# Norm products spread over five steps, and the weight sums of four blocks moved from GpSimd to VectorE

## The chip, the cores and the metric

The kernel runs on one core of a Trainium2 chip. The metric is device time in microseconds (us): 1652.0 us is the median of three runs of the kernel before (1651.32 to 1652.88). Less is better. Five engines execute side by side, each its own list of instructions in order: TensorE (PE, matmuls), VectorE (DVE), ScalarE (ACT), GpSimd (POOL) and SyncE (SP), which here only issues transfers.

## The reference, cut to what matters

One layer of a decoder trunk on a sequence of 1024 tokens with 1024 features, all in float32:

```
mod = silu(c) @ w_ada + b_ada            # six vectors of 1024: shifts, scales, gates
h = rmsnorm(x) * g_mix * (1 + sc1) + sh1
proj = h @ w_in                          # 1024 -> 4640 columns: q, k, v of a dilated attention,
                                         # latents of a second attention, and two gates
x = x + gt1 * (sig(gate_a)*U_a(A) + sig(gate_b)*U_b(B)) @ w_o
h = rmsnorm(x) * g_ffn * (1 + sc2) + sh2
x = x + gt2 * (silu(h @ w_gate) * (h @ w_up)) @ w_down
out = rmsnorm(x) * g_final
```

The change lies in the making of `h` and in the first part of `h @ w_in`.

## The kernel before, in words

**Precision.** A float32 operand is held as two parts, a rounded high part (`hi`, made by ScalarE, L83) and the rest (`lo`, made by VectorE, L84); a product is three matmuls (hi x hi, hi x lo, lo x hi). Each weight tile and each activation tile thus costs one ScalarE cast and one VectorE subtraction before TensorE may use it. The tiles of the split weights are called `Wop`.

**Fast products.** The big matrix products use Strassen's scheme: weight and activation are cut into 2 x 2 quarters, and 7 products replace 8. Each of the 7 needs a sum of weight quarters and a sum of activation quarters. Activation sums are made once (class `Rights`, subtractions at L280, splits into the tiles `cell`). Weight sums are made for every block of weights in `Strassen.left`, by `Strassen.sum` (L192), on the engine named by the class attribute `summer`, which is GpSimd (`POOL`): four sums of 128 x 512 for a block, from `Wraw` (the loaded weights) into `Wsum`. Two of them (S1 and S2) feed products 4 and 5, one feeds 6, one feeds 2; products 0, 1 and 3 use a quarter as it is. The 7 products go in the order 0, 1, 5, 4, 6, 3, 2, each 12 matmuls (L222) into a PSUM bank `bk`. A bank is read by VectorE (L235 adds a base into `x`, L388 makes a finished quarter of the output) before the next product may overwrite it.

**The opening loop** (k from 0 to 7, from L488). For every eighth of the features it loads the modulation weights, makes the norm of the first 512 tokens, multiplies `x` by it (`unit`, L447, "norm products"), applies scale and shift (`affine`, L450), and runs plain products of the first half of 768 columns of `w_in` (six groups of 128, L520). These cover products 0 and 1 of the first six blocks and one output quarter.

**The pair loop** (`for g in range(9)`, L704). The 18 blocks of `w_in` are taken two at a time: pair 0 is blocks 0 and 1, pair 1 blocks 2 and 3, and so on. Blocks 0 to 3 give k and q of the dilated attention. A pair loads its two `Wraw` (1 MB each, L184; there are two buffers, so a load waits until the block before has used its buffer up), and runs products 5, 4, 6, 3, 2 for both. Blocks 0 to 5 come from the opening loop with a base and skip 0 and 1; so do blocks 6 and 7. Between products, chores are put in: the bias table of the attention (one-hot loads L598, matmuls L604, VectorE L605, store L606 into `rxd`, and then eight DRAM-to-DRAM copies of 128 x 1152, L609, into `rxx`), the rotary angles (positions loaded by L613, cast by L618 and on), and the modulation sums (loads L159 from `wada`, VectorE L677, with the condition row `sg` loaded by L666).

**What sets the order.** The program is written in the order above, but a planner places the instructions: it plays the program through with its own clock and gives each engine a list, with hints such as `tc.high_priority` and `tc.issue_after`. After that each engine executes its list strictly in order; an instruction that waits holds everything behind it on its engine.

Of the kernel before, what the change touches and what calls it, by code (L numbers as in the profile page):

```python
# [44 lines left out]
def layer_kernel(ctx: ExitStack, tc: tile.TileContext, xT, c, pos, relT, wada, bada, gains, gq, gkv,  # L45
# [3 lines left out]
    ACT, DVE, PE, POOL, SP = nc.scalar, nc.vector, nc.tensor, nc.gpsimd, nc.sync  # L49
# [5 lines left out]
    def pool(stack, name, bufs=1, **kw):  # L55
        if kw.get("space") is not DRAM:
            kw["reuse_waits"] = "tile"
        return stack.enter_context(tc.tile_pool(name=name, bufs=bufs, **kw))
# [61 lines left out]
    def rms_rows(y, rb, nb=4):  # L120
        for j in range(nb):
            rows_ins[0] = PE.transpose(rb[:, j * P:(j + 1) * P], y[:, j:j + 1].to_broadcast([P, P]), ident)
        return rb
# [279 lines left out]
    with ExitStack() as s0:  # L403
        gwr = pool(s0, "gwr", 3, side="right")
        adap = pool(s0, "adap", 6, side="right")
        early = pool(s0, "early", 1, side="right")
        sqp = pool(s0, "sqp", 3, side="right")
        SQ = lambda: sqp.tile([P, H], F32, name="sq")
        condb = early.tile([P, D], F32, name="condb")
        ssq = [early.tile([P, H], F32, name=f"ssq{i}") for i in range(2)]  # L410
        cr = early.tile([1, D], F32, name="crow")
        badc1 = early.tile([P, 8], F32, name="badc1")
        onesr = early.tile([1, P], F32, name="onesr")
        crow = [cr[:, hsl[hf]] for hf in range(2)]
        for hf in range(2):
            ld(crow[hf], c[:, hsl[hf]])
        for k in range(8):
            ld(x[k][0], xT[k][:, hsl[0]])
        ld(badc, bada)
        ld(gn, gains)  # L420
        DVE.memset(ones1, 1.0)
        DVE.memset(epsc, EPS)
        ACT.activation(warm, ones1, AF.Silu)
        DVE.memset(onesr, 1.0)
        POOL.memset(ident, 0.0)
        POOL.affine_select(ident, ident, pattern=[[-1, P]], compare_op=OP.not_equal, fill=1.0,
                           base=0, channel_multiplier=1)
        sq_ins = [None]

        def square(hf, k):  # L430
            if k == 0:
                ACT.activation(ssq[hf], x[k][hf], AF.Square)
            else:
                q = SQ()
                sq_ins[0] = ACT.activation(q, x[k][hf], AF.Square)
                DVE.tensor_add(ssq[hf], ssq[hf], q)

        def rms(hf):
            ps = trb()
            y = rms_cols([ssq[hf]], D, ps, root=True)  # L440
            rows = rms_rows(y, ps)
            if hf == 1:
                ACT.activation(warm, epsc, AF.Sigmoid)
            return rows

        def unit(k, hf, rb):
            DVE.tensor_mul(x[k][hf], x[k][hf], rb)  # L447

        def affine(out, k, hf):
            return ACT.activation(out, x[k][hf], AF.Identity, bias=modc[:, k:k + 1], scale=Acol[:, k:k + 1])  # L450

        def mod_in(m, k):
            j = m * 8 + k
            t = adap.tile([P, D], F32, name="ada")
            ld(t, wada[j])
            DVE.tensor_tensor_reduce(t, t, condb, 1.0, 0.0, OP.mult, OP.add, modc[:, j:j + 1])
            if m == 1:
                DVE.scalar_tensor_tensor(Acol[:, k:k + 1], modc[:, j:j + 1], badc1[:, k:k + 1], gn[:, k:k + 1],
                                         op0=OP.add, op1=OP.mult)
            else:  # L460
                DVE.tensor_add(modc[:, j:j + 1], modc[:, j:j + 1], badc[:, j:j + 1])

        for k in range(8):
            square(0, k)
            if k == 0:
                for hf in range(2):
                    ACT.activation(crow[hf], crow[hf], AF.Silu)
                    st(cnd[:, hsl[hf]], crow[hf])
                    ps = bank()
                    PE.matmul(ps, onesr, crow[hf], start=True, stop=True)  # L470
                    ins = ACT.copy(condb[:, hsl[hf]], ps)
        with tc.issue_after(sq_ins[0].ins):
            ACT.activation(warm, epsc, AF.Sqrt)
        DVE.tensor_scalar(badc1, badc[:, 8:16], 1.0, None, op0=OP.add)

        def kr_mm(w, t, first, last):
            PE.matmul(pkr[:64], w, t[:, 0], start=first, stop=False, skip_group_check=True)
            PE.matmul(pkr[:32], w[:, :32], t[:, 1], start=False, stop=last, skip_group_check=True)

        def kr_out(t, tmp, hf):  # L480
            ACT.copy(tmp, pkr[32:64])
            DVE.tensor_add(t, pkr[:32], tmp)
            st(krr[:, hsl[hf]], t)

        pss = [bank() for _ in range(NGP)]
        sg = []
        gates = ExitStack()
        for k in range(8):  # L488
            mod_in(1, k)
            mod_in(0, k)  # L490
            if k == 0:
                rb0 = rms(0)
                pkr = trb()
            raw = gwr.tile([P, GW], F32, name="gwraw")
            last = ld(raw, wg0[k])
            if 2 <= k <= 5:
                for kk in (2 * (k - 2), 2 * (k - 2) + 1):
                    with tc.issue_after(last.ins):
                        last = ld(x[kk][1], xT[kk][:, hsl[1]])
            hi = gwr.tile([P, GW + 32], F32R, name="gwh")  # L500
            lo = gwr.tile([P, NGP * P], F32R, name="gwl")
            ACT.copy(hi[:, :GW], raw)
            DVE.tensor_sub(lo, raw[:, :NGP * P], f32(hi[:, :NGP * P]))
            DVE.tensor_sub(hi[:, GW:], raw[:, NGP * P:], f32(hi[:, NGP * P:GW]))
            if k < 4:
                unit(2 * k, 0, rb0)
                unit(2 * k + 1, 0, rb0)
            t = R1.ops[k // 4][k % 4]
            hi_ins = affine(t[:, 0], k, 0)
            affine(x[k][0], k, 0)  # L510
            lo_ins = DVE.tensor_sub(t[:, 1], x[k][0], f32(t[:, 0]))
            if k == 0:
                gates.enter_context(tc.issue_after(hi_ins.ins))
                gates.enter_context(tc.issue_after(lo_ins.ins))
            for j in range(NGP):
                s = slice(j * P, j * P + P)
                if k == 6 and j == 2:
                    gates.enter_context(tc.issue_after(rows_ins[0].ins))
                for n, (wi, ti) in enumerate(((hi, 0), (hi, 1), (lo, 0))):
                    PE.matmul(pss[j], wi[:, s], t[:, ti], start=k == 0 and n == 0, stop=k % 4 == 3 and n == 2,  # L520
                              skip_group_check=True)
            kr_mm(hi[:, NGP * P:], t, k == 0, k == 7)
            if k == 3:
                for j in range(NGP):
                    t = SG()
                    ACT.copy(t, pss[j])
                    sg.append(t)
            if 2 <= k <= 5:
                for kk in (2 * (k - 2), 2 * (k - 2) + 1):
                    square(1, kk)  # L530
            if k == 5:
                with tc.high_priority(offset=400):
                    rb1 = rms(1)
            if k >= 6:
                for kk in range(4 * (k - 6), 4 * (k - 6) + 4):
                    unit(kk, 1, rb1)
        for k in range(8):
            affine(x[k][1], k, 1)
    gates.close()
    gates.enter_context(tc.issue_after(last.ins))  # L540
    prs = [In(j, load=False, base=sg[j]) for j in range(NGP)]
    q6 = In(6, load=False)
    q6.load01()
    tq = pool(ctx, "tq", side="right")
# [177 lines left out]
    with ExitStack() as s2:  # L722
# [293 lines left out]
        for u in range(64 + DEPTH):  # L1016
# [14 lines left out]
            for kp in range(w % 4 + 1) if w >= 0 else ():  # L1031
# [4 lines left out]
                if len(queue) > 2:  # L1036
                    q, k = queue.pop(0)
# [221 lines left out]
    for ci in range(NC):  # L1259
        for dd in range(2):  # L1260
            prs = [Down(2 * dd + e, ops, wnext[:, e]) for e in range(2)]
# [184 lines left out]
```

## Time and profile before

| | before |
|---|---|
| median of 3 runs | 1652.0 us |
| profiled execution, in all | 1657.39 us |
| its span | 1655.5 us |
| mean granted TensorE clock | 0.964 |
| TensorE matmul busy | 1533.7 us (93%) |
| VectorE busy | 1230.6 us (74%) |
| ScalarE busy | 829.9 us (50%) |
| GpSimd busy | 492.1 us (30%) |

Times in the profile are us from the start of its span. In a timeline a row has start, length, engine, line, operation, what is written and read, how many instructions are merged, and in brackets how long the engine was idle just before and what ended the wait. A table of waits has, for each pair of waiter and releaser, the total, the number of times, and the longest. A row of a stretch has its bounds and length, busy time (and count) of TensorE, its weight loads, VectorE, ScalarE and GpSimd, then the granted clock, the transfers' share of their 16 engines, and GB/s.

### The profile page before, as it was taken

How to read it: one execution, taken by the hardware profiler on the slowest of the kernel's cores; microseconds unless marked ns; L12 is line 12 of the kernel's file. 1: busy time of each engine (PE TensorE's matmuls, PEld its weight loads, DVE VectorE, ACT ScalarE, POOL GpSimd, SP SyncE). 2: the span in 40 equal slices, each digit the busy share in tenths (PEclk: the TensorE clock that was granted, in tenths of full speed). 3: DMA queues.
4: the chain of work that ended last, by engine and by line, in shares of the span. 5: the costliest groups of instructions: out<-in, count | busy, mean ns of one | idle time of the engine just before them, and what ended most of it. 6: DMA issues, size and time to landing. Idle time of an engine off the chain costs nothing.

```text
span 1655.5 us, 22260 instructions
## 1 busy us (share of the span) xinstructions
PE 1533.7 (93%) x7306; PEld 1278.2 (77%) x7306; DVE 1230.6 (74%) x2478; ACT 829.9 (50%) x1631; POOL 492.1 (30%) x470
## 2 busy tenths in 40 slices
PE   4988899999778998999999999999999999899996
PEld 2757678877567887899978887778888888788885
DVE  7887898576276766888876569677777677688887
ACT  5742425444366876878744446434444444222325
POOL 0142333223343545433200000423332332233323
PEclk8889999999888999999999999999999999999998
DMA  9439775467996987776376441554444447967512
GB/s 324 185 119 334 239 257 186 142 200 209 281 240 167 225 194 197 175 184 153 90 254 236 126 160 68 180 185 166 165 150 152 166 156 275 396 251 254 187 36 102
DMA packets 175364, 321.40 MB, mean 194 GB/s; under 512 B 36988, under 2 KB 72492, under 8 KB 170000
## 3 DMA queue, kind: packets, MB, share of 16 engines
q1 hardware_dynamic: 107088, 241.22, 42.9%
q0 software_dynamic: 48000, 42.04, 12.0%
q10 hardware_dynamic: 20160, 36.71, 5.9%
q8 instruction: 58, 0.95, 0.2%
q14 instruction: 58, 0.48, 0.1%
HBM read 222.20 MB, written 102.34 MB: 196 GB/s over the span
## 4 chain that ended last, share of the span: by engine, by line
PE 63%; DMA 14%; DVE 12%; ACT 4%; issue 4%; POOL 1%; SPq 0%; ACTq 0%; DVEq 0%; POOLq 0%
PE bk L222 40%; PE acc L894 4%; DMA cell<-ksd 4%; PE S L785 3%; PE bk L87 3%; PE pv L826 3%; PE bk L88 3%; PE bk L89 3%; DMA cell<-nqd 2%; PE tr L807 2%; DVE Wop L84 2%; DMA cell<-tod 1%; PE bk L520 1%; DMA cl<-wada 1%; DVE cell L84 1%
## 5 line engine op out<-in xcount | busy, mean ns | idle before, releaser
L222 PE MATMUL bk<-cell,Wop 128*128 128x512 f32 x4056 | 949.1, 396 | 40.1 <-DVE x L235 14.4
L222 PEld LDWEIGHTS bk<-cell,Wop 128*128 128x128 f32 x4056 | 772.3, 191 | 210.8 <-DVE Wop L84 9.8
L192 POOL TENSOR_TENSOR Wsum<-Wraw 128x512 f32<-128x512 f32 (+1 forms) x116 | 151.7, 1310 | 771.3 <-DVE Wop L84 369.6
L83 ACT CAST Wop<-Wsum 128x512 fp32r<-128x512 f32 (+1 forms) x241 | 129.9, 549 | 222.6 <-PE bk L222 168.7
L83 ACT CAST Wop<-Wraw 128x512 fp32r<-128x512 f32 (+2 forms) x182 | 107.5, 593 | 183.9 <-PE bk L222 101.2
L84 DVE TENSOR_TENSOR Wop<-Wsum,Wop 128x512 fp32r<-128x512 f32 (+1 forms) x241 | 156.4, 657 | 47.0 <-ACT Wop L83 46.2
L84 DVE TENSOR_TENSOR Wop<-Wraw,Wop 128x512 fp32r<-128x512 f32 (+2 forms) x182 | 130.6, 721 | 33.8 <-ACT Wop L83 31.4
L785 PE MATMUL S<-cell,cell 128*128 128x128 f32 (+8 forms) x480 | 120.1, 365 | 12.9 <-DMA cell<-ksd 8.3
L1248 DVE SCALAR_TENSOR_TENSOR x<-bk,modc,x 128x512 f32<-128x512 f32 x140 | 103.7, 748 | 35.9 <-PE bk L222 31.5
L792 ACT ACTIVATE P<-P,mx 128x512 f32<-128x512 f32 (+7 forms) x128 | 99.3, 778 | 35.8 <-DVE mx L787 22.5
L84 DVE TENSOR_TENSOR pl<-tr,ph 128x512 fp32r<-128x512 f32 (+1 forms) x160 | 98.4, 631 | 22.2 <-ACT ph L83 21.2
L894 PE MATMUL acc<-cell,w 128*128 128x512 f32 x408 | 112.2, 403 | 0.1
L807 PE MATMUL tr<-ident,P 128*128 128x128 f32 x576 | 94.5, 282 | 7.1 <-ACT P L795 6.4
L785 PEld LDWEIGHTS S<-cell,cell 96*128 96x128 f32 (+1 forms) x480 | 80.9, 197 | 21.9 <-DMA cell<-ksd 8.7
L192 POOL TENSOR_TENSOR Wsum<-Wraw,Wsum 128x512 f32<-128x512 f32 (+1 forms) x58 | 76.7, 1329 | 65.0 <-DVE Wop L84 62.8
L826 PE MATMUL pv<-ph,v 128*128 128x256 f32 (+1 forms) x320 | 88.2, 293 | 5.9 <-ACT ph L83 5.1
L87 PE MATMUL bk<-cell,Wop 128*128 128x512 f32 (+1 forms) x240 | 91.2, 380 | 1.9 <-ACT Wop L83 1.9
L83 ACT CAST ph<-tr 128x512 fp32r<-128x512 f32 (+1 forms) x160 | 83.3, 544 | 17.2 <-PE tr L807 14.4
L88 PE MATMUL bk<-cell,Wop 128*128 128x512 f32 (+1 forms) x240 | 90.8, 379 | 0.0
L89 PE MATMUL bk<-cell,Wop 128*128 128x512 f32 (+1 forms) x240 | 89.7, 378 | 0.0
L163 ACT COPY x<-bk 128x512 f32<-128x512 f32 x92 | 52.3, 584 | 68.7 <-PE bk L222 45.0
L894 PEld LDWEIGHTS acc<-cell,w 128*128 128x128 f32 x408 | 76.2, 193 | 13.0 <-DVE ev L925 0.3
(255 smaller groups left out, 2181.3 us busy)
## 6 DMA issues: line engine op xcount, KB each, us to landing
tod<-x ACTq DMA_DIRECT2D x140, 256.0 KB, 2.7
cell<-tod SPq DMA_DIRECT2D x70, 512.0 KB, 7.5
Wraw<-win SPq DMA_DIRECT2D x18, 1024.0 KB, 8.0
Wraw<-wgate SPq DMA_DIRECT2D x11, 1024.0 KB
Wraw<-wup SPq DMA_DIRECT2D x11, 1024.0 KB, 6.2
Wraw<-wdown SPq DMA_DIRECT2D x20, 512.0 KB, 4.1
ada<-wada SPq DMA_DIRECT2D x16, 512.0 KB, 6.8
cm<-wada SPq DMA_DIRECT2D x32, 256.0 KB, 3.3
```

Source lines behind the costliest of these rows:

```text
L83: ACT.copy(hi, src)
L84: eng.tensor_sub(lo, src, f32(hi))
L87: PE.matmul(ps, w[0], a[0], start=first, stop=False)
L88: PE.matmul(ps, w[0], a[1], start=False, stop=False)
L89: PE.matmul(ps, w[1], a[0], start=False, stop=last)
L192: self.summer.tensor_tensor(t, a, b, op=op)
L222: PE.matmul(ps, w[:, wi, k], t[k][:, ti], start=start and k == 0 and n == 0, stop=k == self.nk - 1 and n == 2, skip_group_check=True)
L785: anchor[0] = PE.matmul(s, q[:, i * P:i * P + P], k[:, c * wd:c * wd + wd], start=pi == 0, stop=pi == len(passes) - 1)
L807: anchor[0] = PE.transpose(tr[:, co:co + P], self.p[a][:, kb * P:kb * P + P], ident)
L826: anchor[0] = PE.matmul(pv[:, o if l else 0:], v[:, kk], p[:, l:r], start=kk == 0 and n == 0, stop=last and l > 0 and n == 1, skip_group_c ...
L894: PE.matmul(ps, w[wi][:, k0 + k], act(k, ai, hf), start=k == 0 and n == 0, stop=k == nk - 1 and n == 2)
L1248: DVE.scalar_tensor_tensor(xs, self.bk[name], modc[:, 40 + j:41 + j], xs, op0=OP.mult, op1=OP.add)
```

## The change

It has two parts. In the opening loop, `unit` for the first half of the tokens was called twice in each of the steps 0 to 3; now it is called for features (0, 1), (2), (3, 4), (5) and (6, 7) in the steps 0 to 4. And `summer` of blocks 0 to 3 is set to VectorE, so that their 16 sums at L192 are made by VectorE.

```diff
@@ -502,9 +502,8 @@
             ACT.copy(hi[:, :GW], raw)
             DVE.tensor_sub(lo, raw[:, :NGP * P], f32(hi[:, :NGP * P]))
             DVE.tensor_sub(hi[:, GW:], raw[:, NGP * P:], f32(hi[:, NGP * P:GW]))
-            if k < 4:
-                unit(2 * k, 0, rb0)
-                unit(2 * k + 1, 0, rb0)
+            for kk in ((0, 1), (2,), (3, 4), (5,), (6, 7), (), (), ())[k]:
+                unit(kk, 0, rb0)
             t = R1.ops[k // 4][k % 4]
             hi_ins = affine(t[:, 0], k, 0)
             affine(x[k][0], k, 0)
@@ -539,6 +538,8 @@
     gates.close()
     gates.enter_context(tc.issue_after(last.ins))
     prs = [In(j, load=False, base=sg[j]) for j in range(NGP)]
+    for q in prs[:4]:
+        q.summer = DVE
     q6 = In(6, load=False)
     q6.load01()
```

Because a planner places the instructions, more moves than the diff shows. Lines below 505 keep their numbers in the changed kernel, those from L508 to L541 are one lower, and those after it one higher (L618 becomes L619).

**VectorE's list in pair 0, at the first two L235.** `cell` tiles are activation splits, `Wop` weight splits, `x_1035` and `x_1057` the banks read for blocks 0 and 1. Before:

```order
L84 TENSOR_TENSOR Wop_1119<-Wsum_1117,Wop_1119 128x512
L84 TENSOR_TENSOR Wop_1143<-Wraw_1011,Wop_1143 128x512
L84 TENSOR_TENSOR cell9_986<-cl_279,cell9_986 128x512
L84 TENSOR_TENSOR Wop_1165<-Wraw_1013,Wop_1165 128x512
L84 TENSOR_TENSOR cell10_987<-cl_281,cell10_987 128x512
L605 SCALAR_TENSOR_TENSOR cl_1316<-tr_1319,cl_1316 8x512
L84 TENSOR_TENSOR cell11_988<-cm_283,cell11_988 128x512
L235 TENSOR_TENSOR x_1035<-bk_1022,sg_558 128x512
L235 TENSOR_TENSOR x_1057<-bk_1044,sg_560 128x512
```

And now:

```order
L84 TENSOR_TENSOR cell11_988<-cm_283,cell11_988 128x512
L606 SCALAR_TENSOR_TENSOR cl_1316<-tr_1319,cl_1316 8x512
L235 TENSOR_TENSOR x_1035<-bk_1022,sg_556 128x512
L235 TENSOR_TENSOR x_1057<-bk_1044,sg_558 128x512
L84 TENSOR_TENSOR Wop_1119<-Wsum_1117,Wop_1119 128x512
L84 TENSOR_TENSOR Wop_1143<-Wraw_1011,Wop_1143 128x512
L84 TENSOR_TENSOR Wop_1165<-Wraw_1013,Wop_1165 128x512
L192 TENSOR_TENSOR Wsum_1187<-Wraw_1011,Wsum_1017 128x512
L606 SCALAR_TENSOR_TENSOR cl_1468<-tr_1471,cl_1468 8x512
L192 TENSOR_TENSOR Wsum_1211<-Wraw_1013,Wsum_1039 128x512
```

Three weight splits that stood ahead of L235 stand behind it, two sums (L192) are behind it as well, and two others (not in these rows) ahead.

**TensorE's list at the same place**, product 6 of block 0 and the bias matmuls L604. Before:

```order
L222 MATMUL bk<-cell_948,Wop 128x512 x5
L222 MATMUL bk<-cell_969,Wop 128x512 x3
L222 MATMUL bk<-cell_970,Wop 128x512 x3
L222 MATMUL bk<-cell_971,Wop 128x512 x3
L222 MATMUL bk<-cell_972,Wop 128x512 x3
L222 MATMUL bk<-cell_969,Wop 128x512 x3
L222 MATMUL bk<-cell_970,Wop 128x512 x3
L222 MATMUL bk<-cell_971,Wop 128x512 x3
L222 MATMUL bk<-cell_972,Wop 128x512 x3
L604 MATMUL tr<-cl,rt 8x512
L604 MATMUL tr<-cl,rt 8x128
```

And now:

```order
L222 MATMUL bk<-cell_948,Wop 128x512 x5
L605 MATMUL tr<-cl,rt 8x512
L222 MATMUL bk<-cell_969,Wop 128x512 x3
L222 MATMUL bk<-cell_970,Wop 128x512 x3
L222 MATMUL bk<-cell_971,Wop 128x512 x3
L222 MATMUL bk<-cell_972,Wop 128x512 x3
L222 MATMUL bk<-cell_969,Wop 128x512 x2
L605 MATMUL tr<-cl,rt 8x128
```

The two bias matmuls stood behind both blocks' product 6; now one stands ahead of them and one among them.

**VectorE's list in pair 1**, around the second bank read of block 2 (`x_1340`). Before:

```order
L84 TENSOR_TENSOR Wop_1421<-Wsum_1419,Wop_1421 128x512
L84 TENSOR_TENSOR Wop_1445<-Wsum_1443,Wop_1445 128x512
L235 TENSOR_TENSOR x_1340<-bk_1246,sg_562 128x512
L388 TENSOR_TENSOR x_1342<-bk_1286,x_1340 128x512
L84 TENSOR_TENSOR x_1342<-x_1342,x_1344 128x512
L235 TENSOR_TENSOR x_1366<-bk_1268,sg_564 128x512
L388 TENSOR_TENSOR x_1368<-bk_1302,x_1366 128x512
L84 TENSOR_TENSOR x_1368<-x_1368,x_1370 128x512
L388 TENSOR_TENSOR x_1390<-bk_1246,sg_562 128x512
L618 CAST cl_1717<-cl_1717 128x128
```

And now:

```order
L84 TENSOR_TENSOR Wop_1445<-Wsum_1443,Wop_1445 128x512
L619 CAST cl_1717<-cl_1717 128x128
L235 TENSOR_TENSOR x_1340<-bk_1246,sg_560 128x512
L620 TENSOR_SCALAR cl_1717<-cl_1717,fq_69 128x128
L388 TENSOR_TENSOR x_1342<-bk_1286,x_1340 128x512
L621 TENSOR_SCALAR cl_1717<-cl_1717 128x128
```

The cast of the positions, which waits for their load, stood behind the reads of three banks; now it stands ahead of all of them. `x_1340` must be read before TensorE's product 3 of block 2 may start.

## The prediction

> **What bounds the kernel now.** I read the engine shares first, then TensorE's waits in the opening third, then the timelines of TensorE, VectorE and GpSimd there.
>
> ```profile
> PE 1533.7 (93%) x7306; PEld 1278.2 (77%) x7306; DVE 1230.6 (74%) x2478; ACT 829.9 (50%) x1631; POOL 492.1 (30%) x470
> ```
>
> TensorE is the bound on average, so the change can only pay where TensorE stands still. Between 60 and 330 us its waits are:
>
> ```profile
> PE bk L222 <- DVE x L235: 11.7, 3, 5.3
> PE bk L222 <- DVE Wop L84: 4.9, 1, 4.9
> ```
>
> The changed sums themselves appear nowhere in this table; VectorE does. TensorE's timeline (start, length, then idle before) places the waits:
>
> ```profile
> 103.20 1.65 PE L222 MATMUL bk<-cell,Wop 128*128 128x512 f32 x6
> 106.40 1.20 PE L222 MATMUL bk<-cell,Wop 128*128 128x512 f32 x4 [1.55 <-DVE cell L84]
> 112.90 8.19 PE L222 MATMUL bk<-cell,Wop 128*128 128x512 f32 x24 [5.30 <-DVE x L235]
> 121.02 1.24 PE L604 MATMUL tr<-cl,rt 32*8 32x512 f32 x4
> 122.19 38.93 PE L222 MATMUL bk<-cell,Wop 128*128 128x512 f32 x170
> 166.06 4.10 PE L222 MATMUL bk<-cell,Wop 128*128 128x512 f32 x10 [4.94 <-DVE Wop L84]
> 171.75 14.02 PE L222 MATMUL bk<-cell,Wop 128*128 128x512 f32 x60 [1.60 <-ACT Wop L83]
> 188.78 29.52 PE L222 MATMUL bk<-cell,Wop 128*128 128x512 f32 x122 [3.01 <-DVE x L235]
> 221.71 3.78 PE L222 MATMUL bk<-cell,Wop 128*128 128x512 f32 x8 [3.41 <-DVE x L235]
> ```
>
> The six gaps make 19.8 us, all inside the first eight blocks. The long row gives the price of a matmul, 38.93 / 170 = 0.229 us. After a long gap matmuls are slower: 24 took 8.19 where 5.50 is due (2.7 lost), 10 took 4.10 where 2.29 is due (1.8 lost). So a gap costs itself and about 2 us more. Pair 0 (blocks 0 and 1) has 120 matmuls: 48 lie before the 5.30 gap, 24 directly behind it, 48 at the head of the 170. Pair 1 is the next 120 of the 170, pair 2 starts with the last two. Hence pair 0 ends at 122.19 + 48 x 0.229 = 133.2 and the first product (12 matmuls) of pair 2 is complete at 171.75. That is my milestone.
>
> Why is L235 late? VectorE before it:
>
> ```profile
> 88.33 0.67 DVE L84 TENSOR_TENSOR Wop<-Wsum,Wop 128x512 fp32r<-128x512 f32 x1
> 88.93 0.67 DVE L280 TENSOR_TENSOR x<-x 128x512 f32<-128x512 f32 x1
> ...
> 100.37 1.40 DVE L84 TENSOR_TENSOR cell<-cm,cell 128x512 fp32r<-128x512 f32 x1
> 101.69 1.76 DVE L84 TENSOR_TENSOR cell<-x,cell 128x512 fp32r<-128x512 f32 x1
> ...
> 104.59 1.75 DVE L84 TENSOR_TENSOR cell<-chi,cell 128x512 fp32r<-128x512 f32 x1
> 106.27 1.77 DVE L84 TENSOR_TENSOR cell<-x,cell 128x512 fp32r<-128x512 f32 x1
> ...
> 112.18 1.27 DVE L235 TENSOR_TENSOR x<-bk,sg 128x512 f32<-128x512 f32 x2
> ```
>
> VectorE has no gap here: its 33 instructions from 88.33 to 112.18 start 0.60 apart (33 x 0.60 = 19.8), except four that are stretched by 0.73 + 1.09 + 1.08 + 1.10 = 4.0. GpSimd over the same time:
>
> ```profile
> 92.10 10.81 POOL L192 TENSOR_TENSOR Wsum<-Wraw 128x512 f32<-128x512 f32 x2 [23.83 <-DVE Wop L84]
> 104.13 3.36 POOL L192 TENSOR_TENSOR Wsum<-Wraw,Wsum 128x512 f32<-128x512 f32 x2 [1.23 <-DVE Wop L84]
> 114.36 1.43 POOL L192 TENSOR_TENSOR Wsum<-Wraw 128x512 f32<-128x512 f32 x1 [6.86 <-DMA Wraw<-win]
> ...
> 157.03 1.29 POOL L192 TENSOR_TENSOR Wsum<-Wraw 128x512 f32<-128x512 f32 x1 [17.92 <-DMA Wraw<-win]
> ```
>
> The stretched instructions lie exactly where GpSimd's four sums finish and run. Two sums from 92.10 need 10.81 us instead of 2 x 1.43 while VectorE is dense: the two engines exclude each other, first GpSimd waits, then VectorE.
>
> **The change part by part.** *Norm products.* The instruction order of all five engines is the same with and without this part alone, because the planner had already put them two, then six, into VectorE's queue. It costs and brings 0.
>
> *First eight sums (pair 0).* Four move into VectorE's queue at 58 to 67 us, 4 x 0.60 = 2.4, in the places where that queue waits for ScalarE; the eight norm products that follow wait for the same row transposes, and I take 0 (bounds -1 and +1). Two more fall between 88.33 and L235, two behind it. Ahead of L235 the order now has 32 instructions, not 33, since three weight splits went behind it: 88.33 + 32 x 0.60 = 107.6, and GpSimd has nothing left to run. L235 is done at 108.3 instead of 112.85, and TensorE restarts there: **-4.5**. Bounds: -5.3 (the whole gap) and -0.6 (one instruction fewer, the stretches come from something else). The bias matmul L604 that now stands ahead of that restart waits for a one-hot load that is issued when the split of cell9_986 ends, near 105.3; I count it as in time.
>
> With 1.8 lost to the slower clock the 24 matmuls take 7.3, L604's remaining part 0.4, then 48 x 0.229 = 11.0: pair 0 ends at 127.0 instead of 133.2.
>
> *Next eight sums (pair 1).* Their 4.8 us fall where VectorE has had pauses, but each of the first two waits in VectorE's queue for its weight load. Queued behind the first is L235 of block 1, which TensorE needs for its product 3, near 121.9.
>
> ```profile
> 109.31 0.35 SPq L184 DMA_DIRECT2D Wraw<-win  x1
> ...
> 128.42 2.71 SPq L609 DMA_DIRECT2D rxx<-rxd  x4
> ...
> 145.21 0.33 SPq L184 DMA_DIRECT2D Wraw<-win  x1
> 146.00 0.63 SPq L613 DMA_DIRECT2D cl<-pos  x1
> ```
>
> That load took 109.31 to 114.36, 5.05 us. It can now be issued when the fourth sum of block 0 is made, 111.4, and lands near 116.5: 5 us in hand, cost 0 (bound +3).
>
> *What moves with it.* The bias matmuls no longer stand behind the 24, so the bias table's eight big copies (L609) start near 121, 7 us earlier. In the new order the cast L618 of the positions stands *ahead* of L235 of block 2 (x_1340); before, the cast stood seven places behind that L235.
>
> ```profile
> 147.00 0.69 DVE L235 TENSOR_TENSOR x<-bk,sg 128x512 f32<-128x512 f32 x1 [1.30 <-PE bk L222]
> ...
> 157.15 1.25 DVE L618 CAST cl<-cl 128x128 f32<-128x128 int32 x1 [4.00 <-DMA cl<-pos]
> 130.00:145.00 15.00, 15.00 (x68) 12.40 (x67) 13.69 (x24) 5.40 (x9) 4.59 (x3) 1.00 0.97 341
> ```
>
> So TensorE's product 3 of block 2 will wait for the positions. The transfers are saturated there (last row: stretch 130 to 145, share 0.97, 341 GB/s). Positions were issued 17.6 us after the first copy and landed 11.15 later, behind a 1 MB weight load that now stands after them (1.05 MB / 341 GB/s = 3.1). New landing: 121 + 17.6 + 11.15 - 3.1 = 146.7; x_1340 is done 1.25 + 0.69 later, at 148.6. TensorE wants it at 127.0 + 72 x 0.229 = 143.5. A **new gap of 5.1**, plus 1.8 of slow clock. Bounds: no gap (landing before 141.6), and 15.6 (landing at 157.15 as before).
>
> *Pair 2.* Pair 1 ends at 148.6 + 1.8 + 48 x 0.229 = 161.4. Pair 2's weight load (issued 145.21, landed 157.03 before) is issued when the last copy has landed, near 147, with less ahead of it; it takes between 5.05 and 11.8, then two sums of 1.3 and a split pair of 1.3 follow: ready between 156 and 162.7. The gaps of 4.94 and 1.60 thus mostly vanish, and the milestone comes at 161.4 + 2.75 = 164.2, or 165.5 at the late end, instead of 171.75: -7.6 to -6.2.
>
> *Behind it* VectorE is dense up to the L235 of 221.71 and GpSimd still makes the sums there. Same work, same interference: 0, bounds -3 and +3. From 221.71 on TensorE runs dense, so what is gained by then is kept.
>
> **Sum:** I take **-6.5**. The profiled execution (1655.5 span, 1657.4 in all) would become 1650.9; it lies 5.4 above the median of the runs, 1652.0, which becomes **1645.5**.
>
> **The rivals.**
>
> *Slower: the positions land too late.* From the landing T the milestone is T + 1.94 + 1.8 + 11.0 + 2.75 = T + 17.5, so the change loses from T = 154.3. For: the queue is full, and the two broadcast loads (L666) that VectorE also waits for now stand among the copies. Against: 7.6 us of margin. With T as before, 157.15, the milestone is 174.6, +2.9; with two broadcast waits at 2 us more, about +5: **1657**.
>
> *No change: VectorE pays what GpSimd saved.* 16 x 0.60 = 9.6 is added to a queue that is dense from 88 to 112 and from 160 to 222, against stretches of 4.0 that I can show for four sums, at most 16 x 1.1 = 17.6 in all; near 9 the two cancel, the dense stretch to 221.71 ends where it did, and the time is **1652**. For: the last two gaps there wait for VectorE, not for data. Against: none of the added sums lies behind 160. The Trainium skill says this outright: "Perfetto Trace Analysis", Optimizing Scalar/DVE Operations, holds that moving work between GpSimd and VectorE might not help, as they share an SBUF read port. By that rule the result is this rival's 1652; the rows agree on the sharing (92.10 for 10.81), but also show that the price falls on the engine that is late.
>
> *Larger gain: positions in time.* With T below 141.6 the new gap is gone, pair 1 ends at 154.5 and pair 2 waits only for its weights (156 or later): milestone near 159.5, -12: **1640**.
>
> **How the numbers follow.** Forecast (-3.3 to -10) 0.46, larger gain 0.12, no change 0.22, slower 0.20. A measurement of this kernel cannot tell less than 0.2% (3.3 us) from nothing. So faster 0.58, same 0.22, slower 0.20. The range takes in most of the larger gain and of the slow case, 1639 to 1656; the forecast's own is 1642 to 1649.
>
> **What would show it.** Right: no L192 on GpSimd before about 155; VectorE's splits near 100 to 107 all at 0.67; L235 near 108; the gap of 5.30 down to about 2.5; a new TensorE gap near 144 released by L235 with the L618 cast just before it; the gap at 161 gone. Wrong: stretched VectorE instructions without GpSimd beside them; VectorE waiting for `Wraw<-win` at 115 to 122 while TensorE stands; or the gaps before 189 and 222 growing by what was gained.

## The result, and the profile after

The changed kernel takes 1644.1 us (median of 6 runs, 1637.6 to 1647.3) where the kernel before takes 1652.4 on the same chip (6 runs, 1650.4 to 1654.1): ratio **0.9939**, 95% interval 0.9922 to 0.9956. It is faster by about 8 us; the forecast was 1645.5.

The two profiled executions must not simply be subtracted. That of the kernel before took 1657.4, 5.0 above its median; that of the changed kernel took 1637.6 (span 1635.4), 6.5 below its median. So 11.5 of the 19.8 us between them is the luck of two executions.

First the engine totals of the changed kernel (busy us, share of the span, instructions):

```profile
PE 1522.3 (93%) x7306; PEld 1266.9 (77%) x7306; DVE 1227.3 (75%) x2494; ACT 829.1 (51%) x1631; POOL 460.1 (28%) x454
```

Sixteen instructions went from GpSimd (470 to 454) to VectorE (2478 to 2494). GpSimd is busy 32 us less. VectorE is busy 3.3 us *less* with sixteen instructions more; two executions of one program differ by up to 6.7 there (1230.6 before, 1237.3 with the norm products alone), so the number says only that it is no busier. TensorE's timeline after (start, length, then idle before and what ended it; line numbers from L508 on differ by one from those before):

```profile
106.59 1.01 PE L605 MATMUL tr<-cl,rt 32*8 32x512 f32 x2 [1.89 <-DMA cl<-onehot]
107.71 5.03 PE L222 MATMUL bk<-cell,Wop 128*128 128x512 f32 x14
...
112.98 29.78 PE L222 MATMUL bk<-cell,Wop 128*128 128x512 f32 x130
148.53 17.05 PE L222 MATMUL bk<-cell,Wop 128*128 128x512 f32 x66 [5.77 <-DVE x L235]
165.84 12.53 PE L222 MATMUL bk<-cell,Wop 128*128 128x512 f32 x54 [0.27 <-DVE Wop L84]
180.88 28.02 PE L222 MATMUL bk<-cell,Wop 128*128 128x512 f32 x122 [2.50 <-DVE x L235]
212.34 64.90 PE L222 MATMUL bk<-cell,Wop 128*128 128x512 f32 x285 [3.45 <-DVE x L235]
```

The gap of 5.30 us at 112.9 is gone: TensorE goes on at 107.71. A new gap of 5.77 stands at 148.53. Those of 4.94 and 1.60 before pair 2 have shrunk to 0.27. VectorE's and GpSimd's timelines tell why:

```profile
106.89 1.27 DVE L235 TENSOR_TENSOR x<-bk,sg 128x512 f32<-128x512 f32 x2
...
142.26 0.69 DVE L678 CUSTOM_DVE_ANT_0 cm<-cm,sg 128x512 f32<-128x512 f32 x1 [4.02 <-DMA sg<-cnd]
...
147.55 0.23 DVE L619 CAST cl<-cl 128x128 f32<-128x128 int32 x1 [2.52 <-DMA cl<-pos]
147.70 0.68 DVE L235 TENSOR_TENSOR x<-bk,sg 128x512 f32<-128x512 f32 x1
```

```profile
153.17 1.29 POOL L192 TENSOR_TENSOR Wsum<-Wraw 128x512 f32<-128x512 f32 x1 [151.86 <-DVE cl L624]
```

VectorE's L235 pair comes at 106.89, not at 112.18, and GpSimd makes its first sum at 153.17. At 147.70 stands the L235 of block 2 (x_1340), right behind the cast of the positions that waited for its load, and, five microseconds earlier, a product for the modulation (L678) that waited 4.02 for a broadcast load.

### The profile page after: what moved, and what is told of

Same layout as the page of the kernel before. It is cut to its first block, busy times and chain, and to the rows that moved or that the text cites. A ratio compares the mean times of both kernels' runs of the same rounds, so it can differ in the third digit from the quotient of the medians.

```text
span 1635.4 us, 22253 instructions
## 1 busy us (share of the span) xinstructions
PE 1522.3 (93%) x7306; PEld 1266.9 (77%) x7306; DVE 1227.3 (75%) x2494; ACT 829.1 (51%) x1631; POOL 460.1 (28%) x454
## 4 chain that ended last, share of the span: by engine, by line
PE 49%; DMA 5%; DVE 5%; ACT 3%; issue 2%; POOL 1%; ACTq 0%; DVEq 0%; POOLq 0%; SPq 0%
PE bk L222 30%; PE acc L895 3%; PE S L786 3%; PE bk L87 3%; PE bk L89 3%; PE bk L88 3%; PE pv L827 2%; PE tr L808 2%; DMA vbd<-ev 2%; DMA tod<-x 1%; DMA cell<-tod 1%; DVE Wop L84 1%; DMA x<-x1d 1%; DVE cell L84 0%; DVE P L788 0%
## 5 line engine op out<-in xcount | busy, mean ns | idle before, releaser
L222 PE MATMUL bk<-cell,Wop 128*128 128x512 f32 x4056 | 938.0, 392 | 32.3 <-DVE x L235 14.4
L222 PEld LDWEIGHTS bk<-cell,Wop 128*128 128x128 f32 x4056 | 763.5, 189 | 201.4 <-issue 13.2
L192 POOL TENSOR_TENSOR Wsum<-Wraw 128x512 f32<-128x512 f32 (+1 forms) x108 | 131.5, 1220 | 800.0 <-DVE Wop L84 334.0
L786 PE MATMUL S<-cell,cell 128*128 128x128 f32 (+8 forms) x480 | 119.5, 364 | 11.2 <-DMA cell<-ksd 7.0
L192 POOL TENSOR_TENSOR Wsum<-Wraw,Wsum 128x512 f32<-128x512 f32 (+1 forms) x54 | 69.4, 1291 | 59.8 <-DVE Wop L84 57.7
L895 PEld LDWEIGHTS acc<-cell,w 128*128 128x128 f32 x408 | 75.0, 190 | 12.7 <-DVE ev L926 0.3
```

The lines of the kernel that those rows point to most:

```text
L192: self.summer.tensor_tensor(t, a, b, op=op)
L222: PE.matmul(ps, w[:, wi, k], t[k][:, ti], start=start and k == 0 and n == 0, stop=k == self.nk - 1 and n == 2, skip_group_check=True)
L786: anchor[0] = PE.matmul(s, q[:, i * P:i * P + P], k[:, c * wd:c * wd + wd], start=pi == 0, stop=pi == len(passes) - 1)
L895: PE.matmul(ps, w[wi][:, k0 + k], act(k, ai, hf), start=k == 0 and n == 0, stop=k == nk - 1 and n == 2)
```

## The experiments

Each was timed in five rounds against the kernel before on the same chip. "First L361" is a fixed place in the program, the first transposes of line 361, as each profile has it; the kernel before is there at 289.1, the changed kernel at 277.1. That column is from one execution of each kernel, and executions differ: the one of the change with the bias copies later took 7.2 us more than the median of that kernel.

| kernel | ratio | 95% interval | first L361, us |
|---|---|---|---|
| norm products alone | 1.0003 | 0.9988 to 1.0017 | 287.7 |
| sixteen sums alone | 0.9955 | 0.9942 to 0.9967 | 274.3 |
| sums of pair 0 alone | 0.9960 | 0.9946 to 0.9974 | 282.1 |
| sums of pair 1 alone | 0.9999 | 0.9986 to 1.0011 | 287.0 |
| the sixteen sums left out | 0.9918 | 0.9898 to 0.9939 | 274.0 |
| left out, four unread sums on GpSimd | 0.9951 | 0.9932 to 0.9969 | 277.1 |
| change, positions later | 0.9940 | 0.9917 to 0.9963 | 278.4 |
| all sums on VectorE | 0.9976 | 0.9962 to 0.9991 | 276.7 |
| change, bias copies later | 0.9954 | 0.9937 to 0.9971 | 286.1 |
| before, bias copies later | 0.9987 | 0.9974 to 0.9999 | 284.1 |
| change, copies and modulation later | 0.9927 | 0.9900 to 0.9954 | 278.4 |
| change, positions and modulation later | 0.9953 | 0.9938 to 0.9968 | 278.7 |

### The two parts apart

```diff
-            if k < 4:
-                unit(2 * k, 0, rb0)
-                unit(2 * k + 1, 0, rb0)
+            for kk in ((0, 1), (2,), (3, 4), (5,), (6, 7), (), (), ())[k]:
+                unit(kk, 0, rb0)
```

> Part 1 alone: the norm products spread over five steps, all sums left on GpSimd. My theory (the planner had already put them in the same places): ratio 1.000, between 0.998 and 1.002, TensorE waits 5.3 us for L235 near 107 to 113 as before, and no wait changes by over 0.3 us. Rival (spreading them frees VectorE early and carries part of the gain): ratio 0.998 or less, and VectorE's rows before 88 us start earlier.

```diff
+    for q in prs[:4]:
+        q.summer = DVE
```

> Part 2 alone: sixteen sums on VectorE, the norm products as before. My theory: all of the gain, ratio 0.994, between 0.992 and 0.996; the trace shows TensorE restarting near 107.7 and the gap near 143 to 148.5 behind the positions. Rival (the norm products carry part): 0.996 or more.

TensorE's timeline with the norm products alone:

```profile
112.67 8.60 PE L222 MATMUL bk<-cell,Wop 128*128 128x512 f32 x24 [5.31 <-DVE x L235]
...
165.41 4.64 PE L222 MATMUL bk<-cell,Wop 128*128 128x512 f32 x10 [4.21 <-DVE Wop L84]
```

and with the sixteen sums alone:

```profile
105.67 4.77 PE L222 MATMUL bk<-cell,Wop 128*128 128x512 f32 x14
...
146.50 28.84 PE L222 MATMUL bk<-cell,Wop 128*128 128x512 f32 x120 [5.00 <-DVE x L235]
```

The first has the gaps of the kernel before and its time. The second has those of the change, and 0.9955, within the interval of the first. In the traces every engine's instructions stand in the order of the kernel before in the first kernel, and in the order of the change in the second, so the second is a second measurement of the change: 7.4 us by the ratio, 8.5 by the medians (1653.2 and 1644.7). The norm products do nothing; the whole effect is in the sums.

### The sums of one pair alone

```diff
-    for q in prs[:4]:
+    for q in prs[:2]:
         q.summer = DVE
```

> Only the eight sums of blocks 0 and 1 on VectorE; those of blocks 2 and 3 on GpSimd as before. The cast of the positions now stands five places ahead of x_1340 in VectorE's queue. My theory (the dense stretch up to L235 is what costs): TensorE restarts near 107.7 instead of 112.9, 5 us gained; the gap behind the positions is there too, 4 to 7 us near 143 to 149; pair 2's weights come as late as their buffers allow; ratio 0.995 to 0.998. Rival (the second eight sums carry the gain, by freeing GpSimd and the weight buffers): ratio 0.999 or more.

```diff
-    for q in prs[:4]:
+    for q in prs[2:4]:
         q.summer = DVE
```

> Only the eight sums of blocks 2 and 3 on VectorE; those of blocks 0 and 1 on GpSimd as before. The cast of the positions stands two places behind x_1340. My theory: VectorE's stretched rows of 1.4 to 1.8 us between 100 and 108 and the 5.3 us gap stay, TensorE restarts near 112.9; no gap behind the positions; pair 2's 4.9 us wait for Wop shrinks by 2 to 5 us; ratio 0.997 to 1.000. Rival (pair 1's sums carry the gain): ratio 0.995 or less.

TensorE with the sums of pair 0 alone:

```profile
106.69 4.87 PE L222 MATMUL bk<-cell,Wop 128*128 128x512 f32 x14
...
148.55 30.45 PE L222 MATMUL bk<-cell,Wop 128*128 128x512 f32 x120 [5.38 <-DVE cl L622]
182.08 30.83 PE L222 MATMUL bk<-cell,Wop 128*128 128x512 f32 x122 [3.08 <-DVE x L235]
```

VectorE (one of its stretched rows), and then TensorE, with the sums of pair 1 alone:

```profile
101.23 1.76 DVE L84 TENSOR_TENSOR cell<-x,cell 128x512 fp32r<-128x512 f32 x1
```

```profile
112.44 8.32 PE L222 MATMUL bk<-cell,Wop 128*128 128x512 f32 x24 [5.30 <-DVE x L235]
...
162.83 0.73 PE L222 MATMUL bk<-cell,Wop 128*128 128x512 f32 x2 [2.30 <-ACT Wop L83]
```

Pair 0's eight sums bring 0.9960, nearly all. Pair 1's bring nothing that can be measured: the stretched rows and the 5.30 gap stay, and what the weights of pair 2 gain (2.30 here and 1.62 behind it, not 4.94 and 1.60) is small and partly lost again, since the next gap is 3.59 instead of 3.01. With pair 0's alone TensorE is at 148.55, where the whole change is at 148.53. The 5.0 us by which the two differ at the first L361 are, by their rows, nearly all clock: the 122 matmuls take 30.83 behind a gap of 3.08 (granted clock 0.90 from 180 to 215), and 28.02 behind one of 2.50 (1.00 from 180 to 212).

### What the sums cost, and what GpSimd beside VectorE costs

In the first of these kernels the sixteen sums are not made at all; in the second, four sums that nobody reads are put on GpSimd beside VectorE's dense stretch. The lists of the other four engines are the same in both.

```diff
+            if self.summer is None:
+                return self.nosum(op, b)
             t = WS.tile([P, H], F32, name="Wsum")[:, :self.nk * P]
...
+    for q in prs[:4]:
+        q.summer, q.nosum = None, lambda op, b: b
```

> The sixteen sums of blocks 0 to 3 are left out on both engines: the second operand is used in place of each sum, so these blocks' results are not the reference's. It shows what the sums cost VectorE in the change. My theory (on VectorE they lie in time that nothing waits for): TensorE restarts between 105.5 and 107 (two sums fewer ahead of L235 than in the change), and the ratio is 0.991 to 0.995, at most 3 us under the change; the cast of the positions stands behind x_1340's place here, so the gap near 148 is under 3 us. Rival (VectorE pays 9.6 us for the sums): ratio 0.989 or less.

```diff
+    lows = iter(range(4))
+
+    def unread(op, b):
+        lo = f32(R1.ops[5][next(lows)][:, 1])
+        POOL.tensor_tensor(WS.tile([P, H], F32, name="Wsum"), lo, lo, op=op)
+        return b
+
+    prs[0].nosum = unread
```

> As the kernel without the sixteen sums, and GpSimd makes four sums of the same size beside VectorE's dense stretch (92 to 107 us), each waiting only for a split of product 5's operand; nobody reads what they write, and VectorE's and TensorE's lists are the same as without them. My theory (the two engines exclude each other): VectorE's splits in that stretch are held up by 0.7 to 1.1 us each, 2 to 4.5 us in all, TensorE restarts 2 to 4.5 us later than without them, and the ratio is 0.002 higher than without them. Rival (the stretches come from something else): restart and ratio as without them, within 0.5 us and 0.001, and no row over 0.75 us.

Without the sums, VectorE and TensorE:

```profile
105.95 0.67 DVE L235 TENSOR_TENSOR x<-bk,sg 128x512 f32<-128x512 f32 x1
```

```profile
107.10 3.02 PE L222 MATMUL bk<-cell,Wop 128*128 128x512 f32 x12
...
142.94 13.15 PE L222 MATMUL bk<-cell,Wop 128*128 128x512 f32 x50 [2.37 <-DVE x L235]
```

With the four unread sums, GpSimd, VectorE and TensorE:

```profile
94.49 5.50 POOL L548 TENSOR_TENSOR Wsum<-cell 128x512 f32<-128x512 f32 x2 [93.18 <-DVE cell L84]
100.61 1.43 POOL L548 TENSOR_TENSOR Wsum<-cell 128x512 f32<-128x512 f32 x1 [0.62 <-DVE cell L84]
102.66 1.43 POOL L548 TENSOR_TENSOR Wsum<-cell 128x512 f32<-128x512 f32 x1 [0.62 <-DVE cell L84]
```

```profile
97.94 1.14 DVE L84 TENSOR_TENSOR Wop<-Wraw,Wop 128x512 fp32r<-128x512 f32 x1
99.01 1.52 DVE L84 TENSOR_TENSOR cell<-cm,cell 128x512 fp32r<-128x512 f32 x1
...
101.06 1.52 DVE L84 TENSOR_TENSOR cell<-chi,cell 128x512 fp32r<-128x512 f32 x1
...
103.11 1.52 DVE L84 TENSOR_TENSOR cell<-x,cell 128x512 fp32r<-128x512 f32 x1
...
107.57 0.67 DVE L235 TENSOR_TENSOR x<-bk,sg 128x512 f32<-128x512 f32 x1
```

```profile
107.90 1.86 PE L614 MATMUL tr<-cl,rt 32*8 32x512 f32 x2 [4.08 <-DMA cl<-onehot]
109.69 5.49 PE L222 MATMUL bk<-cell,Wop 128*128 128x512 f32 x12
```

This settles the mechanism. Four VectorE rows are stretched, one for each sum, by 0.47 + 3 x 0.85 = 3.0 us; all others take 0.67 as before. Nothing waits for those sums, and no other list differs. This execution ran 1.4 us ahead up to there (TensorE's earlier rows show it), so L235 at 107.57 instead of 105.95 is those 3.0. TensorE makes more of it: it now stands 4.08, not 1.89, for the one-hot load, which is issued behind a VectorE split (at 105.86, not 104.25), and the next 12 matmuls take 5.49 instead of 3.02. Part of that comes back at the next gap, which is 0.57 and not 2.37. At the first L361 this execution is 3.1 us later, 4.5 with its lead counted, and the medians, 1646.5 and 1641.3, are 5.2 apart. The intervals of the two ratios overlap by a little, so how much more than 3.0 it is stays rough. The rival, that the stretches come from something else, is out.

Leaving the sums out gives 0.9918. Against the two measurements of the change (0.9939, 0.9955) that is 3.5 to 6 us, and not all of it is the sums, for here the cast stands behind x_1340 and the gap at 142.94 is 2.37, not 5.77. So by the medians the kernel pays less than 9.6 us for the sixteen sums. 0.9918 lies inside the expected range, but the expected distance to the change, at most 3 us, was exceeded, and TensorE's restart, 107.10, came a tenth of a microsecond late.

### The new gap at 148

```diff
+    def rope_late(t):
+        with tc.issue_after(prs[3].added.ins):
+            rope_run(t)
...
-    cch = [(lambda i=i: bias_load(i), bias_run) for i in range(3)] + [(rope_load, rope_run)]
+    cch = [(lambda i=i: bias_load(i), bias_run) for i in range(3)] + [(rope_load, rope_late)]
```

Here `added` is the instruction of L235.

> The change, and the cast of the positions with what follows it is kept behind block 3's last L235 in VectorE's queue, so it stands behind x_1340. My theory: the gap of 5.0 to 5.8 us near 143 to 148.5 goes or falls under 1.5; pair 2's weights then are late by up to 3 us; TensorE is 2 to 5 us ahead of the change at the gap near 210; ratio 0.991 to 0.994. Rival (pair 2's weights set the time anyway): a new wait for Wop of 4 us or more near 155, and the ratio stays at 0.9945 or more.

VectorE, then TensorE:

```profile
141.42 0.69 DVE L682 CUSTOM_DVE_ANT_0 cm<-cm,sg 128x512 f32<-128x512 f32 x1 [3.91 <-DMA sg<-cnd]
```

```profile
144.95 12.71 PE L222 MATMUL bk<-cell,Wop 128*128 128x512 f32 x48 [3.36 <-DVE x L235]
159.32 4.75 PE L222 MATMUL bk<-cell,Wop 128*128 128x512 f32 x18 [1.66 <-ACT Wop L83]
```

The gap falls from 5.77 to 3.36, not to nothing: x_1340 stood behind *two* waits, and the modulation product that waits for its broadcast load (3.91) is the other one: L235 follows at 144.12. What was won comes back as waits of 1.66 and 0.56 for pair 2's weights. The ratio, 0.9940, is that of the change. Neither side was right as a whole: the gap did not fall under 1.5, and the wait of 4 us for weights that the rival asked for did not come. At the gap near 210 TensorE is 1.3 us ahead of the change (211.07 against 212.34), and 1.2 of that were there at its first L222.

So the modulation products were held back too:

```diff
+    def late(j, ts):
+        with tc.issue_after(prs[3].added.ins):
+            mod_run(j, ts)
...
-    mch += [(lambda j=m * 8 + k: mod_load(j, [CL(), CL()] if j % 2 else None), mod_run) for m in (2, 3, 4, 5) for k in range(8)]
+    mch += [(lambda j=m * 8 + k: mod_load(j, [CL(), CL()] if j % 2 else None), late) for m in (2, 3, 4, 5) for k in range(8)]
```

> The change with the copies where they are, and both the cast of the positions and the products for the modulation kept behind block 3's last L235. My theory (what held x_1340 at 144 in the run with the positions alone was the modulation product that waited 3.91 us for its broadcast load): no gap over 1.5 us for L235 between 140 and 150; pair 2's weights, whose load is still behind the copies, then set the time with waits of 4 to 7 us in all before 170; ratio 0.993 to 0.9955. Rival (x_1340 was the limit, not the weights): weights wait under 2 us, ratio 0.9925 or less.

TensorE's waits for weights from 130 to 230 us (total, times, longest):

```profile
PE bk L222 <- ACT Wop L83: 2.7, 2, 1.7
PE bk L222 <- DVE Wop L84: 2.2, 4, 1.0
```

The first gap for L235 shrinks to 1.34 (at 149.88), and waits for pair 2's weights come instead: 2.7 + 2.2 = 4.9. The ratio stays at 0.9953. Pair 2's weights, not x_1340, are the second limit.

### Are the bias copies the cause behind both?

Positions and pair 2's weights share the transfers with the eight copies of the bias table. They were moved:

```diff
-        if i == 2:
-            for hd in range(NH):
-                st(rxx[hd], dap(rxd, hd * REXT, [[0, P], [1, REXT]]))
...
+        if g == 3:
+            with tc.issue_after(pair[1].loaded.ins):
+                for hd in range(NH):
+                    st(rxx[hd], dap(rxd, hd * REXT, [[0, P], [1, REXT]]))
```

> The change, and the eight big copies of the bias table (4.7 MB in all) are issued behind the weight loads of pair 3 instead of in pair 1, so they no longer fill the transfers from 122 to 147 us. My theory (positions and pair 2's weights are late only because these copies hold the transfers): in the stretch 130 to 165 the transfers' share falls from 0.95 to under 0.8, the gap of 5 to 5.8 us near 148 and the waits for Wop near 158 to 166 go, TensorE is 4 to 8 us ahead of the change at the gap near 210, ratio 0.988 to 0.992. Rival (VectorE sets the pace there, now with the products for the modulation in that stretch as well): a gap of 3 us or more for L235 stays between 130 and 170, ratio 0.993 or more.

The same edit on the kernel before:

> The kernel before, with the same eight copies behind the weight loads of pair 3 and nothing else changed: all sums on GpSimd, norm products as before. My theory (contention and full transfers are two separate causes): the 5.3 us gap for L235 at 112 stays with its stretched VectorE rows, the waits of 4.9 and 1.6 us for pair 2's weights near 161 to 172 go, ratio 0.994 to 0.998. Rival (the full transfers explain the change's gain as well): the gap at 112 shrinks to under 3 us, ratio under 0.993.

And on the change, with the modulation products held back as above:

> The change with the copies of the bias table behind pair 3's weight loads, and the products for the modulation kept behind block 3's last L235 in VectorE's queue. My theory, mended after the last pair of runs (two things hold x_1259 and x_1340 between 130 and 170: transfers filled by the copies, and whatever the planner puts on VectorE in the room that is left): both gone, gaps for L235 between 130 and 170 sum to under 2 us, no Wop wait over 1 us before 175, TensorE completes pair 1 by 152 to 156; ratio 0.988 to 0.993. Rival (the products come due one pair later, where VectorE is dense up to 222 us, and cost there what is saved here): gaps of 4 us or more between 170 and 225 on top of the 2.5 and 3.4 of the change, ratio 0.994 or more.

The change with the copies later: TensorE, and the stretch from 130 to 165 (busy us of TensorE, its weight loads, VectorE, ScalarE, GpSimd; then clock, transfers' share, GB/s):

```profile
144.05 27.56 PE L222 MATMUL bk<-cell,Wop 128*128 128x512 f32 x108 [5.56 <-DVE x L235]
...
183.30 29.37 PE L222 MATMUL bk<-cell,Wop 128*128 128x512 f32 x120 [7.80 <-DVE x L235]
```

```profile
130.00:165.00 35.00, 29.44 (x118) 23.70 (x117) 34.05 (x80) 11.24 (x19) 8.70 (x6) 0.90 0.78 257
```

The transfers' share fell from 0.95 to 0.78 as expected, and the time did not: 0.9954. The planner used the free transfers to pull modulation products forward (17 rows of them from 130 to 165, where the change has 9); VectorE is now busy 34.05 of 35 us, and the gaps for L235 are 5.56 and 7.80. The rival held. On the kernel before, TensorE:

```profile
113.03 8.19 PE L222 MATMUL bk<-cell,Wop 128*128 128x512 f32 x24 [5.31 <-DVE x L235]
...
155.51 0.96 PE L222 MATMUL bk<-cell,Wop 128*128 128x512 f32 x2 [4.11 <-ACT Wop L83]
```

The 5.31 gap does not move when the transfers are freed; a wait of 4.11 for weights comes again, earlier, and the kernel gains 0.13% (interval 0.01 to 0.26), less than the 0.2 to 0.6 that was expected, and a wait for weights was to go that stayed. Contention, not transfers, makes that gap, and the change's gain is not to be had through the transfers. With both copies and modulation later, TensorE:

```profile
143.91 22.05 PE L222 MATMUL bk<-cell,Wop 128*128 128x512 f32 x96 [1.22 <-ACT Wop L83]
173.73 76.83 PE L222 MATMUL bk<-cell,Wop 128*128 128x512 f32 x326 [7.76 <-DVE x L235]
```

Up to 166 the theory is right: one wait of 1.22, no gap for L235. Then the products come due in pair 2 and cost 7.76 in one piece, as the rival said. TensorE reaches the first L361 at 278.4, where the change is at 277.1. The ratio, 0.9927, is the lowest of the kernels that compute everything, but its interval contains that of the change; it is not shown to be better.

### More sums on VectorE

```diff
-        summer = POOL
+        summer = DVE
```

> Every weight sum of the pair loop on VectorE, GpSimd makes none. VectorE gets 56 further sums, 56 x 0.60 = 33.6 us, between 150 and 420, where it was busy 52.7 of 57 us (165 to 222) and 79 of 108 (222 to 330). My theory (what counts is VectorE's place in a dense stretch): the gaps near 189 and 221 grow by 1 to 4 us each, those later do not matter, ratio 0.994 to 1.000, not better than the change. Rival (each sum on GpSimd costs VectorE more than making it itself): ratio 0.993 or less and the gaps near 189 and 221 shrink.

The expectation undercounts: the line is shared by later stages, so 216 further sums moved, 56 in the pair loop and 160 behind it. TensorE with all sums on VectorE:

```profile
361.06 11.09 PE L222 MATMUL bk<-cell,Wop 128*128 128x512 f32 x37 [4.81 <-ACT x L163]
...
1047.36 27.54 PE L222 MATMUL bk<-cell,Wop 128*128 128x512 f32 x120 [1.41 <-ACT x L163]
...
1082.37 17.85 PE L222 MATMUL bk<-cell,Wop 128*128 128x512 f32 x69 [7.48 <-DVE x L235]
```

The same places in the changed kernel:

```profile
359.50 8.41 PE L222 MATMUL bk<-cell,Wop 128*128 128x512 f32 x36 [1.64 <-DVE x L388]
...
1040.05 29.02 PE L222 MATMUL bk<-cell,Wop 128*128 128x512 f32 x120 [4.28 <-ACT x L163]
...
1071.62 6.37 PE L222 MATMUL bk<-cell,Wop 128*128 128x512 f32 x26 [2.56 <-DVE x L235]
```

More brings nothing: 0.9976 is 3.5 to 6 us above the two measurements of the change. The ratio is as expected, the place is not. Up to 277 us the further sums neither help nor hurt (276.7), and the gaps that were to grow did not. At 361 TensorE waits 4.81 where the change waits 1.64. Near 1082 it waits 7.48, but the wait ahead of it shrinks from 4.28 to 1.41, so the two together cost only 2.0 more. Where the rest is lost these profiles cannot tell: the two of the change itself drift apart by 9 us behind the first L361.

## Why the prediction was right, step by step

**Norm products, 0.** Right: 1.0003.

**First eight sums: the stretched rows go, TensorE restarts 4.5 earlier.** Right. L235 is done at 107.6 (forecast 108.3), TensorE goes on at 107.71, 5.2 earlier, of which some 0.7 are there from 76 us on. Counted from TensorE's first L222 (77.17 before, 76.47 after), the first L235 starts 35.0 us on in all four profiles with pair 0's sums on GpSimd, and 30.3 to 30.4 on in the eight with them on VectorE: 4.6 earlier. The clock term held too: 14 matmuls took 5.03 where 3.2 is due, the 1.8 that was set down. The bounds left open whether the stretches were contention; the pair of kernels with unread sums shows that they were. One detail failed: "I count it as in time" of the one-hot load. L605 waited 1.89 for it and was done at 107.6, the same moment as L235; it cost nothing here, but it stands level with L235, and with the unread sums it was the wait that the profile names.

**First four sums in VectorE's early queue, 0; pair 1's sums, 0.** Right within the bounds. VectorE's first sum waited 1.59 for its load. TensorE waited 1.91 and 0.58 near 66 us for the norm in the two profiles of the change, and not at all and 0.52 in the two of the program before, but stood less before its first L222 (0.71 and 0.70, not 1.98 and 2.79). Pair 1's alone measured 0.9999. With pair 0's sums alone the waits before pair 2 are gone as well (120 matmuls run in one piece from 148.55), so that part of the gain too follows from pair 0.

**The new gap.** Forecast 5.1 us, TensorE wanting x_1340 at 143.5 and going on at 148.6; measured 5.77, from 142.76 to 148.53. The positions' load was forecast to land at 146.7 and the cast ran at 147.55.

```profile
122.31 1.22 SPq L610 DMA_DIRECT2D rxx<-rxd  x2
...
136.38 0.61 SPq L614 DMA_DIRECT2D cl<-pos  x1
```

The time is right partly by luck: the load was issued 14.1 behind the first copy, not 17.6, and took 11.2, as long as before (11.15), where 3.1 had been taken off for the weight load that now stands behind it; the two errors cancel. The cause is right only in part: with the cast out of the way the gap is still 3.36, since a modulation product ahead of it waits for its broadcast load. That wait was named among the slower rival's reasons and not in the sum. The size came out right because, besides, the later of the two waits was the one priced.

**Pair 2.** Pair 1's end follows as 148.53 + 1.9 (66 matmuls in 17.05) + 48 x 0.229 = 161.4, and the milestone 2.75 later at 164.2. Both are the forecast's numbers. Against 171.75 before that is -7.6. The prediction calls 171.75 the end of pair 2's first product; that ended at 170.16 (166.06 + 4.10), and 171.75 is the start of the next, behind the wait of 1.60. Now no wait stands there, so as a lead from there on the -7.6 holds.

**Behind it, 0 with bounds of 3.** In these two profiles this is the term that was mis-sized: 4.4 us more lead, outside its bounds. The lead grows from 7.6 to 9.4 at the gap before 212.34, and to 12.0 at the first L361 (289.12 against 277.08). The work is the same; the rows are shorter and the granted clock is higher: the 122 matmuls took 29.52 before and 28.02 after, the 285 took 67.58 and 64.90. The stretch from 165 to 222 before, and then after (clock in the third column from the end):

```profile
165.00:222.00 57.00, 47.93 (x193) 38.30 (x194) 52.67 (x106) 20.08 (x33) 22.45 (x15) 0.93 0.73 251
```

```profile
165.00:222.00 57.00, 50.78 (x222) 40.95 (x221) 55.09 (x115) 18.06 (x30) 24.25 (x16) 1.00 0.80 276
```

The prediction priced the clock behind the gaps that the change moves, and not behind the 3.01 that it shortens to 2.50: 0.5 us of gap and 1.5 of slower rows. The other 2.7, in the 285 matmuls, stand behind a gap that is no shorter (3.41 before, 3.45 after); the change with the positions later took 67.45 there behind 3.41, so this part need not be the change's.

**"What is gained by then is kept".** From the first L361 to the end of the span the thirteen profiles other than that with all sums on VectorE take 1358 to 1368 us, mean 1364, with no relation to how early they get there. So nothing systematic is given back.

**Sum.** -6.5 was forecast; the medians give -8.3, and -8.5 in the second measurement. The two profiles of each program put the lead at the first L361 at 288.4 - 275.7 = 12.7 (means of 289.1 and 287.7, and of 277.1 and 274.3). Some 4 us of that do not show in the medians. Since executions of one kernel spread over up to 10 us, two profiles cannot place them, and it stays open. That 1644.1 fell so near to 1645.5 is in part luck, with the new gap's errors cancelling.

**The rivals.** "VectorE pays what GpSimd saved" is out for pair 0 and fits pair 1 alone (0.9999); the further sums took part of the gain back. The Trainium skill ("Perfetto Trace Analysis", Optimizing Scalar/DVE Operations) holds that moving work between the two engines might not help: the runs disagree where VectorE was dense and late (0.9960, pair 0) and agree elsewhere (0.9999 for pair 1; 0.9976 when 216 more moved). "Positions too late" had its place right and its price not reached: they landed 7 us before the point from which the change would lose. "Positions in time" came nearest in the change with positions and modulation later. With a gap of 1.34 left, pair 2's first product was complete at 160.8 (forecast 159.5), but that was not kept: waits for pair 2's weights cost 3.4 right behind it, and the ratio was 0.9953, some 8 us and not 12.

## What to carry to other kernels

Where GpSimd works beside a dense VectorE, look for single VectorE rows stretched by about one GpSimd instruction, and ask whether the row that TensorE waits for stands behind them; only there did moving the work pay here, and moving more of it did not. In a queue that runs in order, list every wait ahead of the instruction that matters: taking away the last one uncovers the next. Price a gap with the slower matmuls behind it, also where it only shrinks.

## What the runs showed of the hardware that was not expected

*One GpSimd sum, one stretched VectorE row.* The four unread sums held up four 128x512 splits with two inputs, from 0.67 to 1.14 once and to 1.52 three times, and no other row; the first two sums, side by side with VectorE's rows, took 5.50 where two of the later ones (1.43 each) would take 2.9. The Trainium skill ("SBUF — State Buffer", Who interferes with whom) says that a VectorE instruction with two SBUF inputs contends with a GpSimd instruction that reads SBUF, and that what they contend for is an exclusive lock. The trace agrees: four rows were held up for four sums, and the others kept 0.67.

*Gaps and clock.* At one place, the 122 matmuls near 180, eight profiles line up: behind gaps of 2.31, 2.49 and 2.50 us they took 28.0, behind 3.01, 3.06, 3.08, 3.24 and 3.59 they took 29.5, 30.6, 30.8, 29.6 and 30.6. Half a microsecond of gap decides over 1.5 to 2.8 us. The Trainium skill ("TensorE: Matmul & The Clock Gate", Why this matters for your kernels) warns of idle gaps above about 3 us. The trace agrees here, not everywhere: behind a gap of 3.4 the 285 matmuls took 67.6 and 67.5 in two profiles, and 64.9 and 65.3 in two others; behind 2.92 to 2.94 they took 66.2 to 66.4 in three, and behind 2.96 64.9 in another. TensorE's first L222, before and after:

```profile
77.17 7.33 PE L222 MATMUL bk<-cell,Wop 128*128 128x512 f32 x24 [1.98 <-ACT cell L400]
```

```profile
76.47 5.73 PE L222 MATMUL bk<-cell,Wop 128*128 128x512 f32 x24 [0.71 <-ACT cell L400]
```

Here 24 matmuls took 7.3 in the four profiles with a gap of 1.98 to 2.79, and 5.6 to 5.8 in the ten with at most 1.75; the granted clock from 77 to 85 was 0.79 before and 1.00 after.
